# The last store of a row-sum kernel: one DMA on SyncE's queue, or two halves on SyncE's and ScalarE's

## The chip, the cores and the metric

The kernel runs on one core of a Trainium2 chip. The metric is the device time of one execution in microseconds (us); of several runs the median is given.

## The reference

```python
x = np.random.randn(32, 512, 1024).astype(np.float32)
multiplier = 0.5
out = (np.sum(x, axis=-1) * multiplier).astype(np.float32)   # 32 x 512
```

Each of the 16384 rows of 1024 floats is summed and the sum is multiplied by 0.5: 64 MiB are read, 64 KiB are written.

## The kernel before, in words

The 16384 rows are laid over 128 partitions, 128 rows on each, and are loaded in 8 blocks of 16 rows per partition. The first seven blocks (`x_rows`) give 112 results per partition, the last (`x_last`) gives 16. Three buffers `buf` take the blocks in turn. All loads are issued by SyncE (`load`, L75), and a load that reuses a buffer waits for VectorE's semaphore `dve_done`.

Blocks 0 to 5 are summed by VectorE in one reduction each (L117) and scaled into the tile `res` (L123). Block 6 is shared: VectorE sums eight of its rows and ScalarE the other eight, one activation with an accumulator for each row (`act_row`, L82). The last block comes in pieces, so that little is left to do when the last bytes land: rows 0 to 7, 8 to 12, and 13 and 14, then the first 608 elements of row 15 and its other 416 (tile `end`). ScalarE sums seven of these rows (`on_act`), VectorE the rest with `dve_sum` (L92), which multiplies as well. VectorE's last instruction, `final`, adds the sum of the first part of row 15 to that of the second and writes the last column of `res`.

There are two stores. The early one (L150) writes 112 columns of `res` while the last pieces are still on their way. The last one (L175) writes the other 16 columns, 64 bytes on each partition, 8 KB in all. SyncE waits for ScalarE's last row (`act_done`, L174), the store itself waits for `final` (`dve_done`), and SyncE then waits for both stores to land (L179 and L180):

```python
nc.sync.wait_ge(act_done, late_act)
store = nc.sync.dma_start(out=out_last, in_=res[:, own:])
store.wait_op(dve_done, done, "sem-ge")
stored = sem("stored")
store.then_inc(stored, 16)
nc.sync.wait_ge(early_stored, 16)
nc.sync.wait_ge(stored, 16)
```

The order on each engine is the order of the program; no scheduler moves anything, except that the first three loads are put at the program's entry (`start_loads_at_entry`). Engines meet only at semaphores. ScalarE's instructions are one table load and 15 activations; it issues no DMA.

Of the kernel before, what the change touches and what calls it, by code (L numbers as in the profile page):

```python
# [9 lines left out]
def kernel(  # L10
# [13 lines left out]
    nc = tc.nc  # L24
# [4 lines left out]
    P = nc.NUM_PARTITIONS  # L29
# [12 lines left out]
    own = rows - B  # L42
# [3 lines left out]
    out_last = out_flat[P * own : N].rearrange("(p c) -> p c", p=P)  # L46

    def sbuf(name, *shape):
        return ctx.enter_context(nc.sbuf_tensor(name, list(shape), fp32)).ap()
# [4 lines left out]
    res = sbuf("res", P, rows)  # L54
# [4 lines left out]
    def sem(name):  # L59
        return nc.alloc_semaphore(name=name)  # L60

    dve_done = sem("dve_done")
    act_done = sem("act_done")
    counts = {"dve": 0, "act": 0}

    def marks(i, engine):

        s = dve_done if engine == "dve" else act_done
        i.then_inc(s, 1)
        counts[engine] += 1  # L70
        return counts[engine]
# [33 lines left out]
    for b in range(n_blocks - 1):  # L105
# [10 lines left out]
        done = marks(  # L116
            nc.vector.reduce_sum(  # L117
                out=sums[:, c0 : c0 + h], in_=t[:, 0:h, :], axis=mybir.AxisListType.X
            ),
            "dve",  # L120
        )
        freed.append(done)
        scaled = nc.vector.tensor_single_scalar(  # L123
            out=res[:, c0 : c0 + h],
            in_=sums[:, c0 : c0 + h],
# [30 lines left out]
    for k, (lo, hi) in enumerate(pieces):  # L156
# [4 lines left out]
        late_act = marks(i, "act") if k == len(pieces) - 1 else None  # L161
# [9 lines left out]
    final.wait_op(landed_end[1], 17, "sem-ge")  # L171
    done = marks(final, "dve")

    nc.sync.wait_ge(act_done, late_act)  # L174
    store = nc.sync.dma_start(out=out_last, in_=res[:, own:])  # L175
    store.wait_op(dve_done, done, "sem-ge")
    stored = sem("stored")
    store.then_inc(stored, 16)
    nc.sync.wait_ge(early_stored, 16)  # L179
    nc.sync.wait_ge(stored, 16)  # L180

    def start_loads_at_entry(nc_):

# [60 lines left out]
```

## Time and profile before

| what | value |
|---|---|
| time, median of 3 runs | 160.66 us (160.62 to 160.91) |
| span of the profiled execution | 159.4 us |
| median less span | 1.26 us |
| VectorE busy | 119.3 us (75%) |
| ScalarE busy | 17.3 us (11%) |
| DMA queue | 2016 packets, 67.18 MB, 98.0% of 16 engines' span |
| mean rate | 421 GB/s |

The span runs from the first to the last instruction of one profiled execution; the page gives no time of its own for that execution beside it. What lies around the span is in the time and not in the profile. In the rows, SPq is SyncE's sequencer issuing a DMA, ACT is ScalarE and DVE is VectorE. The row of an issue is the time of the sequencer. The transfer itself comes later, and is seen in the share of the 16 DMA engines and in the time from issue to landing.

### The profile page before, as it was taken

Reading aid. Unit: us, or ns where it says so; the run is one execution under the profiler, and the core shown is the slowest. Engines: PE = TensorE matmul, PEld = TensorE weight load, DVE = VectorE, ACT = ScalarE, POOL = GpSimd, SP = SyncE. Lnnn points to the kernel's source line nnn. Section 1 sums busy time; section 2 is a strip of 40 time slices with the busy share of each in tenths; the row PEclk is TensorE's granted clock in tenths of the full one; section 3 lists DMA queues with packets and bytes.
Section 4 is the critical chain, followed back from the end, with each engine's and each line's share of the span. In section 5 each row is a group of like instructions: output and inputs, shape, how many; then the busy total and the mean of one; then the engine's idle time right before and its main releaser. Section 6 shows DMA issues by size and latency. Waiting matters only on the chain.

```text
span 159.4 us, 122 instructions
## 1 busy us (share of the span) xinstructions
DVE 119.3 (75%) x35; ACT 17.3 (11%) x31; POOL 0.2 (0%) x4
## 2 busy tenths in 40 slices
DVE  0000059998699978999599995999959999598644
ACT  3000000000000000000000000000000000397954
POOL 0000000000000000000000000000000000000000
DMA  7996996996999979969969969969979799698994
GB/s 263 526 526 263 526 510 280 526 510 280 526 395 395 526 312 477 526 296 493 526 263 526 526 263 526 510 280 526 477 312 526 345 444 526 280 501 364 421 410 145
DMA packets 2016, 67.18 MB, mean 421 GB/s; under 512 B 480, under 2 KB 608, under 8 KB 736
## 3 DMA queue, kind: packets, MB, share of 16 engines
q1 hardware_dynamic: 2016, 67.18, 98.0%
HBM read 67.11 MB, written 0.07 MB: 421 GB/s over the span
## 4 chain that ended last, share of the span: by engine, by line
DMA 76%; DVE 22%; SPq 1%; issue 0%
DMA xb<-in_x_dram 51%; DMA end<-in_x_dram 25%; DVE sums L117 22%; SPq L75 1%; DVE end L92 1%; DVE res L123 0%; DVE res L92 0%
## 5 line engine op out<-in xcount | busy, mean ns | idle before, releaser
L117 DVE TENSOR_REDUCE sums<-xb 128x16 f32<-128x16384 f32 (+1 forms) x7 | 112.0, 16001 | 30.9 <-DMA xb<-in_x_dram 30.9
L82 ACT ACTIVATE xb<-xb 128x1024 f32<-128x1024 f32 x15 | 15.7, 1044 | 137.7 <-DMA xb<-in_x_dram 137.7
L92 DVE CUSTOM_DVE_ANT_0 xb<-xb 128x512 f32<-128x512 f32 x8 | 5.1, 688 | 4.9 <-DMA xb<-in_x_dram 4.9
L82 ACT ACTIVATION_READ_ACCUMULATOR xb<-xb 128x1 f32 x15 | 2.8, 186 | 0.0
L103 DVE MEMSET end<- 128x2 f32 x1 | 0.1, 60 | 2.5 <-PEq L26 2.5
L82 ACT ACT_TABLE_LOAD x1 | 1.3, 1283 | 2.4 <-PEq L26 2.4
L123 DVE TENSOR_SCALAR res<-sums 128x16 f32<-128x16 f32 (+1 forms) x7 | 1.2, 174 | 0.2
L92 DVE CUSTOM_DVE_ANT_0 end<-end 128x304 f32<-128x304 f32 (+1 forms) x2 | 0.9, 426 | 0.1
L92 DVE DVE_READ_ACCUMULATOR2_ANT res<- 128x1 f32 x9 | 0.7, 82 | 0.0
L225 POOL MEMSET const-bfloat16-1.0<- 128x1 bf16 x1 | 0.1, 102 | 0.0
L225 POOL MEMSET const-uint8-127<- 128x1 uint8 x1 | 0.1, 102 | 0.0
L225 POOL MEMSET const-float32-1.0<- 128x1 f32 x1 | 0.1, 99 | 0.0
L225 POOL MEMSET const-float32-0.0<- 128x1 f32 x1 | 0.1, 98 | 0.2 <-issue 0.2
L92 DVE DVE_READ_ACCUMULATOR2_ANT end<- 128x1 f32 x1 | 0.1, 81 | 0.0
## 6 DMA issues: line engine op xcount, KB each, us to landing
xb<-in_x_dram SPq DMA_DIRECT2D x1, 4096.0 KB, 31.2
xb<-in_x_dram SPq DMA_DIRECT2D x1, 2560.0 KB, 36.9
xb<-in_x_dram SPq DMA_DIRECT2D x1, 1024.0 KB, 38.9
end<-in_x_dram SPq DMA_DIRECT2D x1, 304.0 KB, 39.1
end<-in_x_dram SPq DMA_DIRECT2D x1, 208.0 KB, 39.2
xb<-in_x_dram SPq DMA_DIRECT2D x7, 40.8
out_dram<-res SPq DMA_DIRECT2D x1, 56.0 KB, 10.8
out_dram<-res SPq DMA_DIRECT2D x1, 8.0 KB, 1.4
```

The source lines that it names most:

```text
L75: i = nc.sync.dma_start(out=dst, in_=src)
L82: return nc.scalar.activation(out=t[:, r, :], in_=t[:, r, :], func=mybir.ActivationFunctionType.Copy, scale=mul, accum_out=res[:, col : co ...
L92: return nc.vector.tensor_tensor_reduce(out=row[:, 0:mid], in0=row[:, 0:mid], in1=row[:, mid:], scale=scale, scalar=0.0, op0=ADD, op1=ADD, ...
L103: marks(nc.vector.memset(end[:, at - 2 : at], 0.0), "dve")
L117: nc.vector.reduce_sum(out=sums[:, c0 : c0 + h], in_=t[:, 0:h, :], axis=mybir.AxisListType.X),
L123: scaled = nc.vector.tensor_single_scalar(out=res[:, c0 : c0 + h], in_=sums[:, c0 : c0 + h], scalar=mul, op=mybir.AluOpType.mult,)
L225: nc = _bacc.Bacc("TRN2", target_bir_lowering=False, num_devices=1)
```

## The change

The last store is made by two DMAs of 64 partitions each: partitions 0 to 63 are stored from SyncE's queue and 64 to 127 from ScalarE's. ScalarE gets a wait for its own last row ahead of its DMA, each of the two DMAs waits for VectorE's `final`, each has a semaphore of its own, and SyncE waits for both at the end, besides the early store.

```diff
+    nc.scalar.wait_ge(act_done, late_act)
     nc.sync.wait_ge(act_done, late_act)
-    store = nc.sync.dma_start(out=out_last, in_=res[:, own:])
-    store.wait_op(dve_done, done, "sem-ge")
-    stored = sem("stored")
-    store.then_inc(stored, 16)
+    half = P // 2
+    stored = []
+    for queue, lo in ((nc.sync, 0), (nc.scalar, half)):
+        store = queue.dma_start(
+            out=out_last[lo : lo + half, :], in_=res[lo : lo + half, own:]
+        )
+        store.wait_op(dve_done, done, "sem-ge")
+        stored.append(sem(f"stored{lo}"))
+        store.then_inc(stored[-1], 16)
     nc.sync.wait_ge(early_stored, 16)
-    nc.sync.wait_ge(stored, 16)
+    for s in stored:
+        nc.sync.wait_ge(s, 16)
```

## The prediction

> **What bounds the kernel now.** I read the page first, then the chain that ended last, then the last microseconds in finer and finer views, because the change touches nothing before them. The page:
>
> ```profile
> span 159.4 us, 122 instructions
> ...
> DMA  7996996996999979969969969969979799698994
> ...
> DMA 76%; DVE 22%; SPq 1%; issue 0%
> ...
> out_dram<-res SPq DMA_DIRECT2D x1, 56.0 KB, 10.8
> out_dram<-res SPq DMA_DIRECT2D x1, 8.0 KB, 1.4
> ```
>
> The input stream bounds the kernel: the transfer engines are near full from the first slice to the last but one, and 76% of the chain is loads. The last line is the store that the change divides: 8 KB, 1.4 us from issue to landing, while the larger early store (10.8 us) shares the engines with loads. The chain ends like this (columns: start us, duration us, what):
>
> ```profile
> 117.88 39.13 DMA end<-in_x_dram
> 157.01 0.02 issue
> 157.03 0.50 DVE end L92 x2
> 157.54 0.02 issue
> 157.56 0.38 DVE end L92
> 157.94 0.01 DVE res L92
> ```
>
> The last input piece lands at 157.01, VectorE needs 0.94 us for it, and at 157.95 all sums are in `res`. What follows is not in the chain but in the timeline (start, duration, engine, line) and in SyncE's own waits (total us, times, longest):
>
> ```profile
> 157.23 0.19 ACT L82 ACTIVATION_READ_ACCUMULATOR xb<-xb 128x1 f32 x1
> ...
> 157.86 0.08 DVE L92 DVE_READ_ACCUMULATOR2_ANT res<- 128x1 f32 x1
> 157.97 0.34 SPq L175 DMA_DIRECT2D out_dram<-res  x1
> ```
> ```profile
> SPq L174 <- ACT xb L82: 10.1, 1, 10.1
> SPq L180 <- DMA out_dram<-res: 1.1, 1, 1.1
> ```
>
> SyncE issues the store from 157.97 to 158.31 and then waits 1.1 us for its landing, which ends the span at 159.4. Nothing else runs in this tail of 1.43 us, so any part of it that changes changes the end one for one. ScalarE was done at 157.42, 0.55 us before the store could start. Cut into tenths (us, engines' busy time, clock, share of the transfer engines, GB/s), the tail shows when the store's data moves:
>
> ```profile
> 158.70:158.80 0.10, 0.00 (x0) 0.00 (x0) 0.00 (x0) 1.00 0.00 0
> 158.80:158.90 0.10, 0.00 (x0) 0.00 (x0) 0.00 (x0) 1.00 0.49 46
> 158.90:159.00 0.10, 0.00 (x0) 0.00 (x0) 0.00 (x0) 1.00 0.41 35
> 159.00:159.10 0.10, 0.00 (x0) 0.00 (x0) 0.00 (x0) 1.00 0.02 1
> ```
>
> So the 1.43 us are four parts: 0.34 us issue; about 0.5 us in which nothing moves; some 0.25 us of packets (158.8 to 159.05; 144 of them, by the transfer view of this stretch: 128 of data and 16 that report completion); some 0.35 us until SyncE has the completion and ends.
>
> **What the profiled time is.** The page gives the span, 159.4 us, and no time around it. The median of the three runs is 160.66, so 1.26 us lie outside the span. Nothing outside it is edited: the compiled program of before already declares ScalarE's DMA queue, although it issues nothing on it. I make the sum on the span and add it to 160.66. Differences under 0.2% (0.32 us, about what a measurement of this kernel can tell from no change; the three runs alone spread over 0.29) count as none.
>
> **The change part by part.**
>
> *The new wait on ScalarE.* It waits for its own `act_done`, met at 157.42, and then in the DMA for `dve_done`, met at 157.95. Both are past by 157.97, no instruction is queued behind the DMA on ScalarE, and nobody waits for ScalarE but through the DMA's landing. Cost 0; cover 0.55 us. If ScalarE ended more than 0.55 us later, SyncE's own unchanged wait would be late by the same amount.
>
> *SyncE's half.* Same start, 157.97. Its issue has 64 partitions in place of 128. The trace has only DMAs of 128 partitions, whose issue time does not follow the bytes: 0.35 us for the 56 KB store, 0.34 for the 8 KB one, 0.33 for an 8192 KB load (issued at 97.17). I keep 0.34. This half lands no later than before, so it does not decide unless all of the other's costs vanish.
>
> *ScalarE's half.* It is ready in the same instant, so two issues meet. The nearest rows are SyncE's issues made one right after another (start, duration):
>
> ```profile
> 0.00 0.37 SPq L75 DMA_DIRECT2D xb<-in_x_dram  x1
> ...
> 0.42 0.42 SPq L75 DMA_DIRECT2D xb<-in_x_dram  x1
> ...
> 0.89 0.43 SPq L75 DMA_DIRECT2D xb<-in_x_dram  x1
> ...
> 97.17 0.33 SPq L75 DMA_DIRECT2D xb<-in_x_dram  x1
> ...
> 117.88 0.43 SPq L75 DMA_DIRECT2D end<-in_x_dram  x1
> ```
>
> An issue that stands alone takes 0.33 to 0.35 us, one right behind another 0.42 to 0.47, and their starts are 0.42 and 0.47 apart. That an issue grows longer behind another says that part of it is waiting for something beyond the sequencer that the one before still holds. If ScalarE's sequencer shares that something, its half comes 0.42 to 0.47 later than a lone store would, two issues in a row on two engines. Bounds: below, 0, if the sequencers share nothing; above, 0.47. I take 0.47, since the pair here meets at once. The Trainium skill's page Perfetto Trace Analysis, section DMA Instruction — HWDGE, says that the descriptor generator is shared by two sequencers, locked by one DMA at a time, and that the lock wait lies inside the profiled issue; the longer second rows agree, but no row here has two engines issuing, so it is the rows' pitch that I use.
>
> *First issue of an engine.* ScalarE has issued no DMA before. SyncE's very first issue took 0.37 us against 0.33 alone later: +0.04. That is the near row; the far one is a rival below.
>
> *Packets.* 128 data packets stay, and 16 more report completion: 160 in place of 144. If the halves follow each other, only the second's 80 packets lie on the path: 0.25 x 80/144 = 0.14 us, a gain of 0.11. If they run together, 160 packets take 0.25 x 160/144 = 0.28, a loss of 0.03. The skill's page DMA: Bandwidth & Descriptors, section Rules for kernel authors, speaks against the change: two transfers to disjoint partition halves share the same transfer engines whichever engine issued them, so one transfer of 128 partitions should be used. By that alone there is no gain to be had in the packets, only the loss of 0.03.
>
> *SyncE's waits at the end.* Before, one instruction waits for two semaphores (early store, store). Now there are three, so one more instruction stands at the end. Its price is a step between instructions, 0.02 to 0.05 us in the chain's "issue" rows: +0.04.
>
> Sum: 0.47 + 0.04 - 0.11 + 0.04 = +0.44 us on the span, so 159.4 becomes 159.8 to 159.9, and the time 160.66 + 0.44 = 161.10 us (+0.27%). With the low pitch of 0.42 and no first-issue charge it is +0.35, 161.01; with 0.47 and no gain in packets +0.55, 161.21.
>
> **The rivals.**
>
> *The issues run side by side* (no change). Both sequencers issue in 0.34 us, the packets interleave, and what is left is 0.03 for packets and 0.04 for the wait, perhaps as much again for 16 more completions (my estimate, twice the sum of these two): 160.73 to 160.80. For it: the longer second rows are all on one engine, and may be that engine's own backlog. Against it: SyncE's backlog there is of the same kind of thing that two engines would queue for.
>
> *Fewer partitions make each DMA quicker* (faster). Issue, silence and packets, 0.34 + 0.5 + 0.25 = 1.09 us, may follow the number of descriptors, which is halved on each queue. If all of it did and the queues shared nothing, the gain were 0.55: 160.11 us; if issue and packets alone did, 0.30 less 0.04 for the wait: 160.40. It decides once halving saves more than 0.36 us. For it: no row has fewer than 128 partitions, so nothing in the trace refutes it. Against it: with 7 times the bytes the early store's issue is no longer, so the issue looks fixed; and both queues' packets meet on the same 16 engines.
>
> *ScalarE's issue is dear* (much slower). Its instruction that fetches from outside, ACT_TABLE_LOAD, takes 1.28 us (1283 ns on the page). If a first DMA issue on ScalarE took as long in place of 0.34, the end moves by 0.94: 161.60. It decides as soon as that issue takes over 0.66 us. For it: no issue by ScalarE was seen. Against it: SyncE's first one cost only 0.04 more.
>
> *That the change does not do what it says* is excluded: in the order of instructions of the changed kernel ScalarE's last one is the 64x16 store, behind its 15 activations and waiting on `act_done` and `dve_done`; no load moves on any queue.
>
> **How the numbers follow.** Issues in a row 0.45 (with some 0.05 of it under +0.32 us), dear issue 0.2, side by side 0.22, quicker halves 0.13 (0.01 of it too small to tell). Slower: 0.40 + 0.20 = 0.60. Same: 0.05 + 0.22 + 0.01 = 0.28. Faster: 0.12. Cases of both signs do not hold the middle: the likeliest's own range is 161.0 to 161.2. For 8 in 10 I go down to 160.45, which leaves out most of the quicker case, and up to 161.7, which holds the dear issue to a little over its price.
>
> **What would show it.** In the changed profile everything up to 157.95 should stand as before within the spread. Right: two rows of issue at 157.97, ScalarE's twice as long or ending 0.4 us after SyncE's, packets in two groups, SyncE's last wait about 1.5 us. Side by side: equal rows, one group of some 160 packets, a wait of 1.1 to 1.3. Quicker: rows well under 0.3 us and packets before 158.7. Dear: a ScalarE row near 1 us. The forecast is wrong if the landing of ScalarE's half is less than 0.3 us later than 1.4 us after its issue's start.

## The result, and the profile after

The changed kernel takes 161.32 us (median of 5 runs, 161.20 to 161.49), the kernel before 160.65 (median of 5, 160.62 to 160.91). The ratio is 1.0036, with a 95% interval of 1.0024 to 1.0049: slower, by 0.39 to 0.79 us. The profiled execution took 161.49 us with a span of 160.2, so 1.3 us lie outside the span, as before.

From the page after:

```profile
span 160.2 us, 125 instructions
...
q1 hardware_dynamic: 1952, 67.17, 97.7%
q10 hardware_dynamic: 80, 0.00, 0.0%
...
out_dram<-res SPq DMA_DIRECT2D x1, 56.0 KB, 11.1
out_dram<-res SPq DMA_DIRECT2D x1, 4.0 KB, 1.7
```

There is a second queue now, ScalarE's, with 80 packets, and SyncE's half lands 1.7 us after its issue, where the whole store took 1.4. The listing of transfers has ScalarE's half too (size, us to landing):

```profile
out_dram<-res ACTq DMA_DIRECT2D x1, 4.0 KB, 2.0
```

The end of the chain (start us, duration us, what):

```profile
117.85 39.32 DMA end<-in_x_dram
157.17 0.02 issue
...
157.74 0.38 DVE end L92
158.12 0.01 DVE res L92
```

In this execution the last piece landed 0.16 us later than in the one of before (157.17 against 157.01). That is the load stream: none of its instructions was edited, and the other four runs of the changed kernel have spans 0.2 to 0.3 shorter. From VectorE's end on, the comparison is free of it. The timeline after (start, duration, engine, line):

```profile
158.05 0.08 DVE L92 DVE_READ_ACCUMULATOR2_ANT res<- 128x1 f32 x1
158.16 0.53 SPq L179 DMA_DIRECT2D out_dram<-res  x1
158.16 0.54 ACTq L179 DMA_DIRECT2D out_dram<-res  x1
```

Both issues start in the same instant, as foreseen. They take 0.53 and 0.54 us, where the whole store took 0.34. SyncE's waits, and the stretch cut into pieces of 0.04 us (us, engines' busy time, clock, share of the transfer engines, GB/s):

```profile
SPq L187 <- DMA out_dram<-res: 1.4, 2, 1.2
```
```profile
159.26:159.30 0.04, 0.00 (x0) 0.00 (x0) 0.00 (x0) 1.00 0.00 0
159.30:159.34 0.04, 0.00 (x0) 0.00 (x0) 0.00 (x0) 1.00 0.11 14
...
159.46:159.50 0.04, 0.00 (x0) 0.00 (x0) 0.00 (x0) 1.00 0.14 10
159.50:159.54 0.04, 0.00 (x0) 0.00 (x0) 0.00 (x0) 1.00 0.00 0
...
159.58:159.62 0.04, 0.00 (x0) 0.00 (x0) 0.00 (x0) 1.00 0.18 21
...
159.74:159.78 0.04, 0.00 (x0) 0.00 (x0) 0.00 (x0) 1.00 0.11 8
```

Two separate groups of packets. SyncE's begins at 159.30 to 159.34, some 1.17 us after its issue began. ScalarE's begins at 159.58 to 159.62, some 1.44 after. The whole store's began 0.83 to 0.87 after (in 158.80 to 158.84). So the tail from VectorE's end to the end of the span went from 1.48 us (157.95 to 159.43) to 2.04 (158.13 to 160.17): +0.56 us, well inside the interval of the times. By the completion events in the traces, the whole store landed 1.41 us after its issue began, SyncE's half 1.70 and ScalarE's 1.97. Two things have to be told apart: why the first half is 0.3 late, and why the second is another 0.3 late.

### The profile page after: what moved, and what is told of

Read it like the earlier page. It is cut to its first block, busy times and chain, and to the rows that moved or that the text cites. A ratio compares the mean times of both kernels' runs of the same rounds, so it can differ in the third digit from the quotient of the medians.

```text
span 160.2 us, 125 instructions
## 1 busy us (share of the span) xinstructions
DVE 119.3 (74%) x35; ACT 17.3 (11%) x31; POOL 0.2 (0%) x4
## 4 chain that ended last, share of the span: by engine, by line
DMA 75%; DVE 22%; SPq 1%; issue 0%
DMA xb<-in_x_dram 51%; DMA end<-in_x_dram 25%; DVE sums L117 22%; SPq L75 1%; DVE end L92 1%; DVE res L123 0%; DVE res L92 0%
```

## The experiments

The theory I started from is that the two issues disturb each other (M). The rivals are that a first DMA on ScalarE is dear (C) and that a DMA of 64 partitions is dear by itself (H).

**The halves kept apart in time.** ScalarE does one more activation between VectorE's last sum and its half:

```diff
     nc.scalar.wait_ge(act_done, late_act)
+    pause = nc.scalar.activation(
+        out=t[:, 14, :],
+        in_=t[:, 14, :],
+        func=mybir.ActivationFunctionType.Copy,
+        scale=mul,
+    )
+    pause.wait_op(dve_done, done, "sem-ge")
+    nc.scalar.wait_ge(act_done, marks(pause, "act"))
```

> The changed kernel, but ScalarE does one more activation (about 1.2 us with its waits) between VectorE's last sum and its half of the store, so that the two issues no longer meet. Theory M: both rows go back to 0.33 to 0.36 us and each half's first packet comes 0.8 to 0.9 us after its own issue's start; the time is longer by the pause, about 160.65 + 1.2 to 1.3 = 161.9 to 162.0. Rival C: SyncE's row goes back to 0.34, ScalarE's stays at 0.5 or above. Rival H: both rows stay at 0.5 or above; time 162.3 or more.

Measured: 162.17 us, ratio 1.0084 (1.0067 to 1.0102). Its timeline and its transfers:

```profile
157.90 0.52 SPq L187 DMA_DIRECT2D out_dram<-res  x1
157.90 1.06 ACT L175 ACTIVATE xb<-xb 128x1024 f32<-128x1024 f32 x1 [0.58 <-DVE res L92]
159.04 0.52 ACTq L187 DMA_DIRECT2D out_dram<-res  x1
```
```profile
out_dram<-res SPq DMA_DIRECT2D x1, 4.0 KB, 1.7
out_dram<-res ACTq DMA_DIRECT2D x1, 4.0 KB, 1.7
```

1.14 us lie between the issues, and yet both rows are 0.52 us and both halves land after 1.7. Theory M falls as the cause of the long rows; H stands. The time alone would not have told: 162.17 lies between what M expected (161.9 to 162.0) and what H did (162.3 or more), and the rows decide. What the meeting did cost shows as well: ScalarE's half lands 1.7 after its issue when alone and 2.0 when it meets the other.

**ScalarE's queue used before.** ScalarE loads 4 KB at the start of the program:

```diff
+    warm = sbuf("warm", P, B)
+    warmed = sem("warmed")
+    nc.scalar.dma_start(out=warm[0:64, :], in_=x_rows[0:64, 0, 0:B]).then_inc(warmed, 16)
+    nc.scalar.wait_ge(warmed, 16)
```

> The changed kernel, and ScalarE loads 4 KB on its queue at the very start, so that its half of the store is not its first DMA. Theory M: nothing changes at the end, rows of 0.5 us both, SyncE's first packet after about 1.17 us, ScalarE's after 1.44; time 161.2 to 161.5 like the changed kernel. Rival C: ScalarE's row falls to 0.35 and the time to 160.7 to 161.0. The early load's own row is ScalarE's first issue without a second one beside it at the same instant, if SyncE's entry issues are over by then: 0.35 by theory M, 0.5 or more by rival C.

Measured: 161.32 us, ratio 1.0029 (1.0018 to 1.0041), the same as the changed kernel within the intervals. The timeline has the early load's issue at 2.38 with 0.54 us, and at the end

```profile
158.04 0.53 SPq L183 DMA_DIRECT2D out_dram<-res  x1
158.05 0.53 ACTq L183 DMA_DIRECT2D out_dram<-res  x1
```

ScalarE's row goes from 0.54 to 0.53: being first cost about 0.01 to 0.02 us. Rival C falls. That M expected the same time here is no support for it: M wanted 0.35 us for the early load's row, which met no other issue, and it took 0.54. C wanted 0.5 or more there, but H accounts for that row as well, since the early load also has 64 partitions.

**The whole store from ScalarE.**

```diff
-    nc.sync.wait_ge(act_done, late_act)
-    store = nc.sync.dma_start(out=out_last, in_=res[:, own:])
+    nc.scalar.wait_ge(act_done, late_act)
+    store = nc.scalar.dma_start(out=out_last, in_=res[:, own:])
```

> The whole last store, 128 partitions, from ScalarE's queue; SyncE issues no last store. Theory M (two issues that meet disturb each other through something that both sequencers share): ScalarE issues alone, so its row is 0.33 to 0.36 us, the first packet comes 0.8 to 0.9 us after the issue's start and the landing after about 1.45 us; time 160.6 to 160.8, no change. Rival C (a first DMA on ScalarE is dear by itself): the row stays at 0.5 to 0.6 us as in the changed kernel, first packet after 1.1 to 1.4 us, time 160.9 to 161.3.

Measured: 160.77 us against 160.75 of before in the same session, ratio 0.9999 (0.9990 to 1.0008), no change.

```profile
157.75 0.37 ACTq L175 DMA_DIRECT2D out_dram<-res  x1
```
```profile
out_dram<-res ACTq DMA_DIRECT2D x1, 8.0 KB, 1.4
```

ScalarE's first and only DMA takes 0.37 us to issue where SyncE takes 0.34, and lands as soon. Neither the engine nor its queue is dear.

**Both halves from SyncE.**

```diff
-    nc.scalar.wait_ge(act_done, late_act)
...
-    for queue, lo in ((nc.sync, 0), (nc.scalar, half)):
+    for queue, lo in ((nc.sync, 0), (nc.sync, half)):
```

> Two halves, both from SyncE's queue, one behind the other. Theory M: the first row is 0.34 us and its packets start at 0.84 us as for a lone store, the second row starts some 0.42 to 0.47 us later; the end moves by 0.3 to 0.45 us: 160.95 to 161.1, somewhat better than the changed kernel or equal to it. Rival H (a DMA of 64 partitions is dearer than one of 128): the first row is already longer than 0.4 us and its first packet comes after 1.0 us or later; time 161.3 or more.

Measured: 161.66 us, ratio 1.0053 (1.0037 to 1.0068).

```profile
157.81 0.53 SPq L178 DMA_DIRECT2D out_dram<-res  x1
158.39 0.58 SPq L178 DMA_DIRECT2D out_dram<-res  x1
```

The first of the two has nothing beside it when it is issued and still takes 0.53, as H said, and its first packet comes 1.17 us after its start (158.98). The second starts 0.58 later, not 0.42 to 0.47. Both land 1.7 us after their start, so two halves issued 0.58 us apart do not hold each other up by 0.3.

**One half alone.** One store of partitions 0 to 63 from SyncE (`out=out_last[0:64, :], in_=res[0:64, own:]` in the kernel before).

> One store from SyncE as in the kernel before, but of partitions 0 to 63 alone; the last 16 columns of the other 64 partitions are left out. If a DMA of 64 partitions is dearer by itself (as the paused kernel's rows of 0.52 us and first packets after 1.17 us say), the time is 0.25 to 0.35 us above the kernel before, 160.9 to 161.1, though half the bytes are stored. If halves were dear only beside another half, the time would be that of before or a little under, 160.5 to 160.75.

Measured: 161.04 us against 160.76, ratio 1.0019 (1.0009 to 1.0029).

```profile
157.75 0.53 SPq L175 DMA_DIRECT2D out_dram<-res  x1
```

Its landing takes 1.7 us. Half the bytes cost 0.28 us more.

**Which counts are dear.** Ten stores in a row behind the last one, each waiting for the one before, so that from start to start is the time to land and wake SyncE:

```diff
+    shapes = [(0, 128, 16), (0, 112, 16), (0, 96, 16), (0, 64, 16), (64, 128, 16), (0, 32, 16), (0, 16, 16), (0, 128, 8), (0, 64, 8), (0, 128, 16)]
+    for k, (lo, hi, w) in enumerate(shapes):
+        again = sem(f"again{k}")
+        nc.sync.dma_start(
+            out=out_last[lo:hi, 0:w], in_=res[lo:hi, own : own + w]
+        ).then_inc(again, 16)
+        nc.sync.wait_ge(again, 16)
```

> The kernel before, followed by ten more stores of the same sums from SyncE, each after the one before has landed: 128, 112, 96, 64 (lower), 64 (upper), 32 and 16 partitions of 64 bytes, then 128 and 64 partitions of 32 bytes, then 128 of 64 bytes again. Only the rows of these stores are of interest, not the time. Theory F (any count but 128 pays a fixed step): 128 takes 0.34 us to issue and about 1.4 to land, all others 0.52 and about 1.7. Theory G (the price follows the count): 112 and 96 lie between 0.34 and 0.52, and 32 and 16 above 0.52. Theory B (it is the bytes): 128 partitions of 32 bytes take 0.52 as 64 of 64 bytes do.

The timeline of one execution, in the order of the list, from 112 partitions to 64 of 32 bytes:

```profile
160.82 0.35 SPq L184 DMA_DIRECT2D out_dram<-res  x1
...
162.23 0.32 SPq L184 DMA_DIRECT2D out_dram<-res  x1
...
163.62 0.53 SPq L184 DMA_DIRECT2D out_dram<-res  x1
...
165.33 0.47 SPq L184 DMA_DIRECT2D out_dram<-res  x1
...
166.99 0.32 SPq L184 DMA_DIRECT2D out_dram<-res  x1
...
168.35 0.32 SPq L184 DMA_DIRECT2D out_dram<-res  x1
...
169.68 0.35 SPq L184 DMA_DIRECT2D out_dram<-res  x1
...
171.11 0.47 SPq L184 DMA_DIRECT2D out_dram<-res  x1
```

| partitions | issue, us | start to next start, us |
|---|---|---|
| 128 | 0.33 | 1.42 |
| 112 | 0.35 | 1.41 |
| 96 | 0.32 | 1.39 |
| 64 (lower) | 0.53 | 1.71 |
| 64 (upper) | 0.47 | 1.66 |
| 32 | 0.32 | 1.36 |
| 16 | 0.32 | 1.33 |
| 128, 32 bytes each | 0.35 | 1.43 |
| 64, 32 bytes each | 0.47 | 1.65 |

All three theories written down for this run fell (a fixed step for any count but 128, a price by the count, the bytes). 64 alone is dear. Every other count is level with 128 or a little quicker: 0.09 us from 128 to 16.

**How far this goes.** The same with other shapes; the list of DMAs, in order: stores of 80, 64, 48, 64 (from partition 32) and 8 partitions of 64 bytes, of 64 and 128 partitions of 448 bytes, loads of 64, 96 and 128 times 64 bytes.

```diff
+    spare = sbuf("spare", P, rows)
+    shapes = [
+        (out_last[0:80, :], res[0:80, own:]),
+        (out_last[0:64, :], res[0:64, own:]),
...
+        (spare[:, 0:B], x_rows[:, 0, 0:B]),
+    ]
...
```

> The kernel before, followed by ten more DMAs from SyncE, each after the one before has landed: stores of 80, 64, 48, 64 (partitions 32 to 95) and 8 partitions of 64 bytes, then of 64 and of 128 partitions of 448 bytes, then loads of 64, 96 and 128 pieces of 64 bytes. Only the rows are of interest. Theory S: the three stores of 64 and the load of 64 take 0.46 to 0.53 us to issue, all others 0.32 to 0.36. If only multiples of 32 or powers of two matter, 8 is dear too; if the dearness belongs to a start at partition 0 or 64, the one from 32 is not dear; if it belongs to small packets, the one of 448 bytes is not; if it belongs to stores, the load of 64 is not.

Issue rows of one execution, in that order: 0.35, 0.56, 0.33, 0.57, 0.33, then 0.48 and 0.36, then 0.51, 0.32 and 0.35 us. Four of them, 64 partitions and 48, 64 from partition 32, and the load of 64:

```profile
160.89 0.56 SPq L198 DMA_DIRECT2D out_dram<-res  x1
...
162.63 0.33 SPq L198 DMA_DIRECT2D out_dram<-res  x1
...
163.99 0.57 SPq L198 DMA_DIRECT2D out_dram<-res  x1
...
170.31 0.51 SPq L198 DMA_DIRECT2D spare<-in_x_dram  x1
```

The four of 64 are dear by 0.12 to 0.25 us over their neighbours, wherever they start, with either size of packet, stores and load alike; 80, 48 and 8 are not. From start to start, 64 stored partitions of 64 bytes take 1.74 and 1.77 against 1.39 for 80 and 1.36 for 48. The expectation (0.46 to 0.53) held in kind; two rows went above it.

**What the meeting costs.** Six pairs behind the last store, one DMA from each engine at once, each pair after the one before has landed:

```diff
...
+    for k, two in enumerate(pairs):
+        both = []
+        for queue, (o, i) in zip((nc.sync, nc.scalar), two):
+            for s in before_pair:
+                queue.wait_ge(s, 16)
+            both.append(sem(f"pair{k}_{len(both)}"))
+            queue.dma_start(out=o, in_=i).then_inc(both[-1], 16)
+        before_pair = both
...
```

> The kernel before, followed by six pairs of stores, one from SyncE and one from ScalarE at the same instant, each pair after the one before has landed; in order: 128 and 128 partitions, 64 lower and 64 upper, 64 upper and 64 lower, 128 and 64, 64 and 128, 128 and 128. Only the rows are of interest. If meeting costs the second about 0.27 us and the first nothing, as in the changed kernel against the paused one: of each pair one lands as alone (1.4 us for 128, 1.7 for 64) and the other some 0.3 later, whatever the shapes; SyncE's and ScalarE's rows stay near 0.35 (128) and 0.53 (64). If the meeting costs more with 128 partitions, whose 144 packets are more, the second of 128 and 128 lands 0.4 or more later.

The rows of pairs two to five (64 and 64, 64 and 64, 128 and 64, 64 and 128):

```profile
161.11 0.53 SPq L197 DMA_DIRECT2D out_dram<-res  x1
161.12 0.55 ACTq L197 DMA_DIRECT2D out_dram<-res  x1
...
163.16 0.47 SPq L197 DMA_DIRECT2D out_dram<-res  x1
163.17 0.49 ACTq L197 DMA_DIRECT2D out_dram<-res  x1
...
165.19 0.34 SPq L197 DMA_DIRECT2D out_dram<-res  x1
165.20 0.47 ACTq L197 DMA_DIRECT2D out_dram<-res  x1
...
166.92 0.47 SPq L197 DMA_DIRECT2D out_dram<-res  x1
166.94 0.37 ACTq L197 DMA_DIRECT2D out_dram<-res  x1
```

From SyncE's start to its next start, a pair of 64 and 64 takes 2.05 and 2.03 us, against 1.71 and 1.66 for one of 64 alone. A pair of 128 and 64 takes 1.73, of 64 and 128 1.67 (166.92 to the sixth pair's 168.59): as one of 64 alone. So "some 0.3 later, whatever the shapes" was wrong. Only when two of 64 meet is one of them 0.3 late. It was ScalarE's each time, in the changed kernel, with its queue used before and in both pairs here, and each time SyncE's issue had started first, by 0.014 us at most. Whether the later one loses or ScalarE's does stays open.

Two of 128 cost less. The first pair started 0.12 us askew, ScalarE ahead; from ScalarE's 159.41 to the next 161.12 it took 1.71, the skew included, against 1.42 for one of 128. The sixth started together, and from its start to the end of the span 1.61 us pass (168.59 to 170.20), against 1.46 behind the last single store of 128 in the list above (172.76 to 174.22).

**The same split by columns.** Each DMA has all 128 partitions and 8 of the 16 columns:

```diff
-    half = P // 2
+    half = B // 2
...
-    for queue, lo in ((nc.sync, 0), (nc.scalar, half)):
+    for queue, lo in ((nc.sync, 0), (nc.scalar, B // 2)):
...
-            out=out_last[lo : lo + half, :], in_=res[lo : lo + half, own:]
+            out=out_last[:, lo : lo + half], in_=res[:, own + lo : own + lo + half]
```

> Two DMAs on two queues as in the changed kernel, but each of all 128 partitions and half of the 16 columns. If the count of 64 partitions is what made both halves late, rows are 0.34 and 0.37 us, SyncE's first packet comes after 0.84 us, and only the cost of meeting is left, 0.27 us or somewhat more for twice the packets: 160.9 to 161.1, less than the changed kernel's 161.3. If meeting is most of it, the time is 161.2 or more.

Measured: 160.97 us against 160.76, ratio 1.0008 (0.9999 to 1.0017).

```profile
158.33 0.34 SPq L179 DMA_DIRECT2D out_dram<-res  x1
158.33 0.38 ACTq L179 DMA_DIRECT2D out_dram<-res  x1
```

The landings take 1.4 and 1.6 us. With the count back at 128, most of the loss is gone. The times alone could not tell what is left from nothing, but the trace shows where it lies. SyncE's first packet comes at 159.17, 0.84 us after its issue began, as for a lone store, and ScalarE's at 159.22, 0.89 after, where alone, with the whole store, it came 0.87 after. So two issues of 128 that meet do not queue. Their packets are over at 159.37 and 159.42. SyncE's 16 completions then arrive from 159.57 to 159.73, and ScalarE's only behind them, from 159.74 to 159.90.

**The same split at partition 96.**

```diff
-    for queue, lo in ((nc.sync, 0), (nc.scalar, half)):
+    for queue, lo, hi in ((nc.sync, 0, 96), (nc.scalar, 96, P)):
...
-            out=out_last[lo : lo + half, :], in_=res[lo : lo + half, own:]
+            out=out_last[lo:hi, :], in_=res[lo:hi, own:]
```

> The changed kernel with the cut at partition 96 in place of 64: SyncE stores partitions 0 to 95, ScalarE 96 to 127. Theory S (what is dear is a DMA of exactly 64 partitions, since 128, 112, 96, 32 and 16 all took 0.32 to 0.35 us to issue): SyncE's row 0.32 and first packet after 0.81, ScalarE's row 0.35 and first packet after 0.84 to 0.9; what is left is that two times 16 completions come in one after another, which put the second landing at 1.57 in the kernel by columns, so the last landing comes after 1.40 to 1.57 us: time 160.6 to 160.9. Rival (two DMAs of parts of the partitions on two queues disturb each other whatever their size): 161.2 to 161.5 as in the changed kernel.

Measured: 160.95 us against 160.75, ratio 1.0011 (1.0002 to 1.0020), a little above the expected 160.9.

```profile
158.00 0.36 SPq L178 DMA_DIRECT2D out_dram<-res  x1
158.01 0.39 ACTq L178 DMA_DIRECT2D out_dram<-res  x1
```
```profile
out_dram<-res SPq DMA_DIRECT2D x1, 6.0 KB, 1.4
out_dram<-res ACTq DMA_DIRECT2D x1, 2.0 KB, 1.6
```

Two queues, two parts of the partitions, two issues in the same instant, and the time is 0.37 us under the changed kernel's (161.32 - 160.95). Neither part is 64. Against 160.75, the median of 15 runs of the kernel before, the changed kernel's loss is 0.57 us; its 0.67 is against the median of 5 runs, 160.65. What is left, 0.2 us, is ScalarE's 1.6 in place of 1.4. The kernel by columns leaves the same, and in the same place: here too ScalarE's completions (159.42 to 159.60) come behind SyncE's (159.24 to 159.43). No version tried beats the kernel before; one store from either engine is the best.

## Why the prediction was right, and where it was not

The time (161.32, forecast 161.10 in 160.45 to 161.7) and the sign were right. The sum was +0.44 us. The median moved by 0.67, or 0.57 against the 160.75 of the sessions with more runs, and the tail of the profiled executions by 0.56. The mechanism was right in part, and that the sum came near is partly luck. Of the signs that the prediction named, the two groups of packets came; ScalarE's row neither was twice as long as SyncE's nor ended 0.4 us after it (0.54 against 0.53, from the same start). The terms:

- **SyncE's half** was taken to land no later than the whole store. This step failed. It lands after 1.70 us and not 1.41. A DMA of 64 partitions is issued in 0.53 us and not 0.34, and from the end of its issue to its first packet another 0.64 pass (158.69 to 159.32) and not 0.49 (158.32 to 158.81); its packets win back some 0.03. The term was put at 0 although no row had other than 128 partitions; it is +0.3. The rival of quicker halves had its place right (the count of partitions) and its sign wrong.
- **Two issues in a row** was put at 0.47, the pitch of SyncE's rows. In the changed kernel the second half's packets come 0.27 us after the first's, not 0.47. ScalarE's row is not longer for the meeting, either: 0.54 against 0.52 for the half kept apart. The delay lies after the row, between the issue's end and the first packet. The Trainium skill's page Perfetto Trace Analysis, section DMA Instruction — HWDGE, puts the wait for the shared generator inside the profiled issue; these rows do not show it there. And it needs two DMAs of 64: a 64 beside a 128 loses nothing, and two of 128 begin their packets 0.05 us apart. So the mechanism as forecast, two ordinary issues queueing, was not what happened. Two terms, 0 and 0.47, stood where 0.3 and 0.27 belonged, and that their sums are close is luck.
- **First issue of ScalarE**, +0.04: about 0.02 (0.54 against 0.53 with the queue used before). That a whole store takes it 0.37 us where SyncE takes 0.34 is not from being first: its sixth DMA of the pairs, also of 128, takes 0.37. The dear issue, a chance of 0.2 and 161.60, did not occur. Its price was taken from ACT_TABLE_LOAD, and no run shows that this instruction has anything in common with a DMA issue.
- **Packets**, -0.11: two groups, as the forecast's case had them. The second lasts from about 159.60 to 159.78, 0.18 us, against about 0.21 (158.81 to 159.02) for the whole store's one, so the gain was 0.03. The 0.25 of the forecast came from windows of a tenth, too coarse for it, and the time does not follow the number of packets: 80/144 of 0.21 would have been 0.12.
- **SyncE's extra wait**, +0.04: nothing. It waits for the first half while the second is still on its way (two waits, 1.4 us together, the longer 1.2), and the span ends 0.04 us behind the last landing (160.13 to 160.17), as before (159.39 to 159.43).
- **ScalarE's new wait**, 0: right, its row starts with SyncE's.

The Trainium skill's page DMA: Bandwidth & Descriptors, section Rules for kernel authors, advises against two transfers to disjoint partition halves since they share the engines; the advice was right here, 161.32 against 160.65. Its reason is the small part, though: cut at 96 in place of 64, with the same sharing, it costs 0.20 us and not 0.57 (both against 160.75).

What stays open is why 64 is dear, and what two DMAs of 64 share. The runs show where the time lies (0.12 to 0.25 in the issue, and 0.3 by the first packet) and that neither bytes, number of packets, start partition, direction nor engine makes it. The other counts stand on few rows each, 112, 80, 48, 16 and 8 on a single one, and no other count between 48 and 80 was run.

## What to carry to other kernels

The small store at the end of this kernel costs about 1.4 us that hardly depend on its size between 1 and 8 KB, so cutting it in two buys nothing: from 128 to 16 partitions the landing comes 0.09 us sooner, and a second DMA cost 0.2 here. Before estimating a DMA of a new shape from rows of another, measure the shape: one kernel that issues a list of shapes at its end, each after the last has landed, gives the whole table in one run. When the forecast and the time agree, check the rows all the same; here two wrong terms made a nearly right sum.

## What the runs showed of the hardware that I had not expected

- A DMA of exactly 64 partitions from SyncE or ScalarE takes 0.47 to 0.58 us to issue. One of 128, 112, 96, 80, 48, 32, 16 or 8, alone from SyncE, took 0.32 to 0.36 in the two lists. A small store of 64 lands about 0.3 us later than one of 16 to 128.
- When two DMAs of 64 start together, ScalarE's lands 0.3 us later than alone and SyncE's does not; beside one of 128, one of 64 lands as alone.
- When two DMAs of 128 start together, or of 96 and 32, their packets begin 0.05 us apart, and the second's completions come behind the first's: 1.6 us in place of 1.4.
- The issue time hardly grows when two engines issue in the same instant: 0.53 and 0.54 us against 0.52 apart, for 64 partitions; 0.34 and 0.38 against 0.34 and 0.37, for 128. The most seen is 0.36 against 0.32, for 96 beside 32.
- A store of 8 partitions comes back sooner than one of 16: 1.16 us from start to start (165.75 to 166.91) against 1.33.
